# Sliding windows by scatter: identity shuffles in place of VectorE copies, and another buffer for a final tile

## The chip, the cores and the metric

The kernel runs on one core of a Trainium2 chip. The metric is the device time of one execution in microseconds (us), as the median of several runs. Profiles come from one execution each, with all times counted from the start of its span.

## What is computed

The input `x` is 16 x 64 x 64 x 64 float32 (batch, channel, row, column). The output holds, for each of 15 x 15 window positions, the 8 x 8 window of every channel; windows step by 4 rows and columns, so they overlap by half.

```python
n_h = (h - window_size) // stride + 1      # 15
n_w = (w - window_size) // stride + 1      # 15
for i in range(n_h):
    for j in range(n_w):
        result[:, i, j] = x[:, :, 4*i:4*i + 8, 4*j:4*j + 8].copy()
```

Nothing is calculated. The input has 16.8 MB and the output 59.0 MB: 3600 rows (batch, i, j) of 64 x 8 x 8 float32, 16 KB each.

## The kernel before

**Input.** The tile `L` keeps the whole input in the on-chip memory. A partition stands for a half of the channels (`ch`, partitions 0 to 63 or 64 to 127), one of two groups of eight batches (`y`), a batch and a quarter of the image's rows (`q`); it has 32 channels x 16 rows x 64 columns. Sixteen loads of a `(ch, y, q)` each, eight of them split over two queues, are issued by SyncE (SP) and GpSimd (POOL). A window's upper edge lies in one of four slots `s` of a quarter; windows of slots 0 to 2 lie inside the quarter, and those of slot 3 take their lower four rows from the next partition.

**Output tiles.** Four buffers `G0` to `G3` of 128 partitions x 64 x 8 x 8 are used in turn: `tile_()` counts `at` up and gives `G[(at - 1) % 4]`. A tile is filled by copies on ScalarE (`act`) and VectorE (`dve`), each of which takes a strided 8-column piece out of `L`, and is then sent by `scatter` (L123), an indirect DMA on POOL's queue that gives each partition a row of the output by an index tile. Indices beyond the bound mark rows that are left out. A buffer is filled again when its last store has landed, so three tiles can be under way while the fourth is filled.

**The order.** It is written out by hand:

- `part` (L166): six tiles of slots 0 and 1 of two columns of windows, eight copies of 32 partitions each; they need only half of the input (`y`), so that the first three go out while the other half loads.
- `unit(j, 0)`, the plain tile: `fill` makes four copies of 64 partitions x 2048 elements (L143), two on ScalarE and two on VectorE. There are eight, the first three between the later `part` tiles.
- `unit(j, 2)`, the cross tile: one half of the partitions gets slot 2 by two ScalarE copies (L143), the other half gets slot 3 by VectorE: for each channel half a copy of the upper four rows (L145, 64 x 1024) and a `stream_shuffle` of the lower four rows from the next partition (L146, 64 x 1024, mask `nxt`). 16 of its 128 rows are left out. There are 15.
- From the fourth plain tile on three cross tiles and a plain tile alternate, five times.
- At the end the last column's slots 0 and 1 make two tiles of 64 partitions (L212): two copies on ScalarE and two on VectorE fill one, and four plain DMAs of 256 KB (L215) send it. The first tile's four DMAs are on SP's queue, the second's alternate between SP and ScalarE.

Counted from 0, tiles 0 to 8 are the `part` tiles and the first three plain ones, 9 to 28 the five rounds. `at` is 29 then; with the `at += 1` in the final loop, its two tiles get the buffers of tiles 25 and 27 (`G1` and `G3`).

POOL executes its scatters in order, each after the copies that fill its tile. ScalarE and VectorE execute their copies in order and wait, at a tile's first copy, for its buffer's last store. The stores are declared to be independent of each other.

Of the kernel before, what the change touches and what calls it, by code (L numbers as in the profile page):

```python
# [10 lines left out]
def kernel(  # L11
# [7 lines left out]
    nc = tc.nc  # L19
# [11 lines left out]
    CH = 2  # L31
# [6 lines left out]
    HP = P // CH  # L38
# [79 lines left out]
    def free(st):  # L118
        tc.declare_no_dep(st.ins, group="stores", reason="each store writes rows of its own")
        tc.add_to_no_dep_group("stores", st.ins)  # L120

    def scatter(g, ix, j, s):
        st = nc.gpsimd.indirect_dma_start(  # L123
            out=o_v,
            out_offset=bass.IndirectOffsetOnAxis(ap=ix[:, 0:1], axis=0),
            in_=g.rearrange("p c r w -> p (c r w)"),
            in_offset=None,
            element_offset=(s * NW + j) * CFREE,
            bounds_check=B * NWIN - 1,
            oob_is_err=False,  # L130
        )
        free(st)

    def fill(g, half, s, j, lo, n, copies):

        d = slice(half * HP + lo, half * HP + lo + n)
        cols = slice(j * ST, j * ST + WS)
        for ch in (half, 1 - half):
            f = slice(ch * HP + lo, ch * HP + lo + n)
            cs = slice(ch * CL, (ch + 1) * CL)  # L140
            copy = copies[ch != half]
            if s < NSLOT - 1:
                copy(out=g[d, cs, :, :], in_=L[f, :, s * ST : s * ST + WS, cols])  # L143
            else:
                copy(out=g[d, cs, 0:ST, :], in_=L[f, :, s * ST : RB, cols])  # L145
                nc.vector.stream_shuffle(out=g[d, cs, ST:WS, :], in_=L[f, :, 0:ST, cols], mask=nxt)  # L146

    act, dve = nc.scalar.copy, nc.vector.tensor_copy


    EARLY = 3
    at = 0

    def tile_():
        nonlocal at
        at += 1
        return G[(at - 1) % NG]

    def part(y, j):
        g = tile_()  # L160
        for d in range(P // QP):
            s, dj = d // NY, d % NY
            cols = slice((j + dj) * ST, (j + dj) * ST + WS)
            for ch in range(CH):
                f = (ch * NY + y) * QP
                (act if (2 * d + ch) % 3 == 0 else dve)(  # L166
                    out=g[d * QP : (d + 1) * QP, ch * CL : (ch + 1) * CL, :, :],
                    in_=L[f : f + QP, :, s * ST : s * ST + WS, cols],
                )
        scatter(g, (idx_y0, idx_y1)[y], j, 0)  # L170

    crossed = 0

    def unit(j, s):
        nonlocal crossed
        g = tile_()
        if s == 0:
            for half in range(CH):
                fill(g, half, half, j, 0, HP, (act, dve))
            scatter(g, idx, j, s)  # L180
        else:

            turn = crossed % 2
            crossed += 1
            fill(g, turn, s, j, 0, HP, (act, act))
            fill(g, 1 - turn, s + 1, j, 0, HP, (dve, dve))
            scatter(g, (idx_hi, idx_lo)[turn], j, s)

    for n in range(EARLY):
# [1 line left out]
    plain = [(j, 0) for j in range(2 * EARLY, NW - 1)]  # L191
    cross = [(j, 2) for j in range(NW)]
    for n in range(EARLY):
        part(1, 2 * n)
        unit(*plain.pop(0))
    while plain:
        for w in cross[:3]:
            unit(*w)
        cross = cross[3:]
        unit(*plain.pop(0))  # L200


    j = NW - 1
    for s in range(2):
        g = tile_()
        at += 1
        cols = slice(j * ST, j * ST + WS)
        for y in range(NY):
            d = slice(QP + y * QP, QP + (y + 1) * QP)
            for ch, copy in enumerate((act, dve)):  # L210
                f = slice(ch * HP + y * QP, ch * HP + (y + 1) * QP)
                copy(out=g[d, ch * CL : (ch + 1) * CL, :, :], in_=L[f, :, s * ST : s * ST + WS, cols])  # L212
        g_q = g.rearrange("p c r w -> p (c r w)")
        for q in range(HQ):
            free((nc.sync, nc.scalar)[s * q % 2].dma_start(out=o_q[q * NSLOT + s, j], in_=g_q[QP + q : QP + q + (B - 1) * HQ + 1 : HQ]))  # L215
# [35 lines left out]
```

## Time and profile before

| | |
|---|---|
| median of 8 runs | 192.09 us (191.96 to 192.33) |
| the profiled execution | 192.27 us, of which its span is 190.5 |
| scatters (L123) | 29; issue to landing 8.0 to 16.4 us, median 13.7 |
| scatter packets (16 KB) | 3472 |
| ScalarE copy, 2048 elements | 1896 ns |
| VectorE copy of 2048, of 1024 elements | 1225 ns, 688 ns |
| VectorE shuffle of 1024 elements | 1275 ns |
| scatter on POOL | 0.96 to 2.2 us |

A line of the profile's groups names the line of code, the engine, the operation and its output and input with their shapes, then how many there were, their busy time in us and the mean of one in ns, and the idle time of the engine in front of them with what ended most of it. A line of the timeline has the start and the duration in us, the engine, the line and the operation; in brackets the idle time before it and what ended it. "SPq" and "ACTq" are DMA issues on these queues. The DMA row of the page is the mean busy share of 16 DMA engines in 40 equal slices of the span, in tenths, where 9 stands for 90% or more.

### The profile page before, as it was taken

Reading aid. Unit: us, or ns where it says so; the run is one execution under the profiler, and the core shown is the slowest. Engines: PE = TensorE matmul, PEld = TensorE weight load, DVE = VectorE, ACT = ScalarE, POOL = GpSimd, SP = SyncE. Lnnn points to the kernel's source line nnn. Section 1 sums busy time; section 2 is a strip of 40 time slices with the busy share of each in tenths; the row PEclk is TensorE's granted clock in tenths of the full one; section 3 lists DMA queues with packets and bytes.
Section 4 is the critical chain, followed back from the end, with each engine's and each line's share of the span. In section 5 each row is a group of like instructions: output and inputs, shape, how many; then the busy total and the mean of one; then the engine's idle time right before and its main releaser. Section 6 shows DMA issues by size and latency. Waiting matters only on the chain.

```text
span 190.5 us, 481 instructions
## 1 busy us (share of the span) xinstructions
DVE 120.5 (63%) x160; ACT 130.0 (68%) x69; POOL 49.8 (26%) x50
## 2 busy tenths in 40 slices
DVE  4000007999998969877749586795877679455220
ACT  0000007999999979977779589797877979487250
POOL 7402203205635321522322222223122432210000
DMA  2999999999999999999999999999999999999974
GB/s 84 318 405 401 400 399 398 399 400 395 420 437 423 418 420 427 427 403 434 437 403 427 421 421 416 423 430 416 420 423 420 416 427 427 408 423 434 413 337 169
DMA packets 11156, 75.81 MB, mean 398 GB/s; under 512 B 3456, under 2 KB 3456, under 8 KB 7552
## 3 DMA queue, kind: packets, MB, share of 16 engines
q0 software_dynamic: 9040, 66.34, 84.7%
q1 hardware_dynamic: 2048, 8.91, 12.0%
q10 hardware_dynamic: 64, 0.52, 0.7%
q14 instruction: 4, 0.03, 0.0%
HBM read 16.78 MB, written 62.91 MB: 418 GB/s over the span
## 4 chain that ended last, share of the span: by engine, by line
DMA 84%; DVE 6%; ACT 3%; POOL 2%; issue 1%; ACTq 0%; DVEq 0%; PEldq 0%
DMA out_dram<-G,idx_hi 30%; DMA L<-in_x_dram 21%; DMA out_dram<-G,idx 14%; DMA out_dram<-G,idx_y 13%; DMA out_dram<-G,idx_lo 7%; DVE G L166 4%; POOL L L58 2%; ACT G L212 2%; ACT G L143 1%; DVE G L146 1%; DVE G L145 0%; DVE G L143 0%; POOL pi L69 0%; ACTq L143 0%; DVEq L145 0%
## 5 line engine op out<-in xcount | busy, mean ns | idle before, releaser
L143 ACT COPY G<-L 64x2048 f32<-64x2048 f32 x46 | 87.2, 1896 | 16.9 <-DMA out_dram<-G,idx_hi 7.6
L166 DVE COPY G<-L 32x2048 f32<-32x2048 f32 x30 | 36.7, 1222 | 29.3 <-DMA L<-in_x_dram 26.3
L146 DVE STREAM_SHUFFLE G<-L 64x1024 f32<-64x1024 f32 x30 | 38.3, 1275 | 0.0
L166 ACT COPY G<-L 32x2048 f32<-32x2048 f32 x18 | 33.9, 1896 | 1.3 <-DMA out_dram<-G,idx_y 1.0
L145 DVE COPY G<-L 64x1024 f32<-64x1024 f32 x30 | 20.6, 688 | 16.6 <-DMA out_dram<-G,idx_hi 10.4
L143 DVE COPY G<-L 64x2048 f32<-64x2048 f32 x16 | 19.6, 1225 | 6.6 <-DMA out_dram<-G,idx 6.3
L166 ACT ACT_TABLE_LOAD x1 | 1.3, 1283 | 29.8 <-DMA L<-in_x_dram 29.8
L123 POOL DMA_INDIRECT out_dram<-G,idx_y x6 | 10.9, 1810 | 25.1 <-DVE G L166 15.6
L58 POOL DMA_DIRECT2D L<-in_x_dram x16 | 11.0, 696 | 24.4 <-DMA L<-in_x_dram 23.9
L123 POOL DMA_INDIRECT out_dram<-G,idx_hi x8 | 9.6, 1200 | 24.1 <-DVE G L146 15.3
L123 POOL DMA_INDIRECT out_dram<-G,idx_lo x7 | 8.1, 1152 | 29.3 <-DVE G L146 19.6
L123 POOL DMA_INDIRECT out_dram<-G,idx x8 | 10.0, 1254 | 18.3 <-ACT G L143 18.3
L212 ACT COPY G<-L 32x2048 f32<-32x2048 f32 x4 | 7.6, 1896 | 5.5 <-DMA out_dram<-G,idx_hi 5.5
L212 DVE COPY G<-L 32x2048 f32<-32x2048 f32 x4 | 5.1, 1280 | 8.0 <-DMA out_dram<-G,idx_hi 7.9
L72 DVE TENSOR_SCALAR tb<-pi 128x1 int32<-128x1 int32 x1 | 0.2, 153 | 1.0 <-POOL pi L69 1.0
L78 DVE TENSOR_TENSOR th<-tc,tq 128x1 int32<-128x1 int32 x2 | 0.3, 156 | 0.0
L75 DVE TENSOR_SCALAR th<-tc 128x1 int32<-128x1 int32 x2 | 0.3, 154 | 0.0
L69 POOL IOTA pi<- 128x1 int32 x1 | 0.1, 125 | 0.4 <-PEq L246 0.4
L146 DVE LOAD_MASK_SELECT G<-L x30 | 0.2, 7 | 0.0
L78 DVE CUSTOM_DVE_ANT_0 idx_y<-idx_y,idx 128x2 uint16<-128x2 uint16 x1 | 0.2, 159 | 0.0
L78 DVE CUSTOM_DVE_ANT_0 idx_lo<-tb,th 128x2 uint16<-128x2 uint16 x1 | 0.2, 159 | 0.0
L78 DVE CUSTOM_DVE_ANT_0 idx<-tb,th 128x2 uint16<-128x2 uint16 x1 | 0.2, 159 | 0.0
(16 smaller groups left out, 2.2 us busy)
## 6 DMA issues: line engine op xcount, KB each, us to landing
L<-in_x_dram POOLq DMA_DIRECT2D x8, 1024.0 KB, 21.2
L<-in_x_dram SPq DMA_DIRECT2D x8, 896.0 KB
out_dram<-G SPq DMA_DIRECT2D x6, 256.0 KB
L<-in_x_dram POOLq DMA_DIRECT2D x8, 128.0 KB, 21.3
out_dram<-G ACTq DMA_DIRECT2D x2, 256.0 KB
out_dram<-G,idx POOLq DMA_INDIRECT x8, 14.9
out_dram<-G,idx_hi POOLq DMA_INDIRECT x8, 14.6
out_dram<-G,idx_lo POOLq DMA_INDIRECT x7, 12.9
```

The lines of the kernel that those rows point to most:

```text
L58: eng.dma_start(out=L[p0 : p0 + QP - HQ + 1 : HQ, c0:c1, :, :], in_=x_v[ch, y, q, :, c0:c1, :])
L69: nc.gpsimd.iota(pi[:, :], pattern=[[0, 1]], base=0, channel_multiplier=1)
L72: nc.vector.tensor_scalar(out=d[:, :], in0=pi[:, :], scalar1=shift, scalar2=mask, op0=ALU.logical_shift_right, op1=ALU.bitwise_and)
L75: nc.vector.tensor_scalar(out=d[:, :], in0=a[:, :], scalar1=float(m), scalar2=None, op0=ALU.mult)
L78: nc.vector.tensor_tensor(out=d[:, :], in0=a[:, :], in1=b[:, :], op=op)
L123: st = nc.gpsimd.indirect_dma_start(out=o_v, out_offset=bass.IndirectOffsetOnAxis(ap=ix[:, 0:1], axis=0), in_=g.rearrange("p c r w -> p (c ...
L143: copy(out=g[d, cs, :, :], in_=L[f, :, s * ST : s * ST + WS, cols])
L145: copy(out=g[d, cs, 0:ST, :], in_=L[f, :, s * ST : RB, cols])
L146: nc.vector.stream_shuffle(out=g[d, cs, ST:WS, :], in_=L[f, :, 0:ST, cols], mask=nxt)
L166: (act if (2 * d + ch) % 3 == 0 else dve)(out=g[d * QP : (d + 1) * QP, ch * CL : (ch + 1) * CL, :, :], in_=L[f : f + QP, :, s * ST : s * S ...
L212: copy(out=g[d, ch * CL : (ch + 1) * CL, :, :], in_=L[f, :, s * ST : s * ST + WS, cols])
```

## The change

A second VectorE helper moves rows by a shuffle whose mask maps each partition to itself, so that the same data is moved as by a copy. A third, `mix`, gives the first quarter of the channels of a piece to a ScalarE copy and the rest to such a shuffle. In the plain tiles from the fourth on VectorE's two copies of 2048 elements become a shuffle of 2048 and a `mix` (ScalarE 512, VectorE 1536). In the cross tiles VectorE's two copies of 1024 elements become a shuffle of 1024 and a `mix` (ScalarE 256, VectorE 768); the two shuffles with the mask `nxt` stay. The first three plain tiles, the `part` tiles and the final two keep their copies.

The count of buffers at the end changes as well: one buffer is passed over ahead of the final loop and none within it, so that its two tiles get the buffers of tiles 26 and 27 (`G2` and `G3`).

```diff
     act, dve = nc.scalar.copy, nc.vector.tensor_copy
+    same = list(range(32))
+
+
+    def shf(out, in_):
+        nc.vector.stream_shuffle(out=out, in_=in_, mask=same)
+
+    def mix(out, in_):
+        k = out.shape[1] // 4
+        act(out=out[:, 0:k], in_=in_[:, 0:k])
+        shf(out=out[:, k:], in_=in_[:, k:])
...
-    def unit(j, s):
+    def unit(j, s, fast=False):
         nonlocal crossed
         g = tile_()
         if s == 0:
-            for half in range(CH):
-                fill(g, half, half, j, 0, HP, (act, dve))
+            fill(g, 0, 0, j, 0, HP, (act, dve if fast else shf))
+            fill(g, 1, 1, j, 0, HP, (act, dve if fast else mix))
             scatter(g, idx, j, s)
         else:
...
             fill(g, turn, s, j, 0, HP, (act, act))
-            fill(g, 1 - turn, s + 1, j, 0, HP, (dve, dve))
+            fill(g, 1 - turn, s + 1, j, 0, HP, (shf, mix))
             scatter(g, (idx_hi, idx_lo)[turn], j, s)
...
         part(1, 2 * n)
-        unit(*plain.pop(0))
+        unit(*plain.pop(0), fast=True)
...
     j = NW - 1
+    tile_()
     for s in range(2):
         g = tile_()
-        at += 1
         cols = slice(j * ST, j * ST + WS)
```

## The prediction, made before the changed kernel ran

> **What bounds the kernel now.** I read the page's busy line and its 40 slices first, to see which resource is full.
>
> ```profile
> DVE 120.5 (63%) x160; ACT 130.0 (68%) x69; POOL 49.8 (26%) x50
> ...
> DMA  2999999999999999999999999999999999999974
> GB/s 84 318 405 401 400 399 398 399 400 395 420 437 423 418 420 427 427 403 434 437 403 427 421 421 416 423 430 416 420 423 420 416 427 427 408 423 434 413 337 169
> ```
>
> No compute engine is full; the DMA engines are at 9 in every slice between the first and the last two. The windows view of 2 us stretches says whether the dips in GB/s are idle time (columns: length, busy us and count of DVE, ACT and POOL, PEclk, DMA share, GB/s).
>
> ```profile
> 110.00:112.00 2.00, 1.24 (x2) 1.26 (x2) 0.14 (x1) 1.00 1.02 430
> 112.00:114.00 2.00, 1.97 (x2) 1.98 (x2) 1.24 (x1) 1.00 0.99 418
> 114.00:116.00 2.00, 0.57 (x2) 1.88 (x2) 0.07 (x1) 1.00 0.98 401
> 116.00:118.00 2.00, 1.97 (x4) 1.98 (x2) 1.32 (x1) 1.00 1.08 459
> ```
>
> They are not: the share stays within some hundredths of 1.00, and GB/s swings only by which window a 16 KB packet starts in. The trace's DMA records give the 3472 scatter packets 0.611 us at the least and 0.624 on average, with 16 of them in flight on average in every 2 us from 48 to 179 us. The steady part is bound by the transfers. Third, the groups, for the prices:
>
> ```profile
> L146 DVE STREAM_SHUFFLE G<-L 64x1024 f32<-64x1024 f32 x30 | 38.3, 1275 | 0.0
> ...
> L145 DVE COPY G<-L 64x1024 f32<-64x1024 f32 x30 | 20.6, 688 | 16.6 <-DMA out_dram<-G,idx_hi 10.4
> L143 DVE COPY G<-L 64x2048 f32<-64x2048 f32 x16 | 19.6, 1225 | 6.6 <-DMA out_dram<-G,idx 6.3
> ```
>
> VectorE waits for stores to release buffers (10.4 and 6.3 us above), not the stores for VectorE. Last, the timeline, for one plain tile (from 111.84) and for the end (the four large copies of ScalarE at 111.83 are of two tiles).
>
> ```profile
> 111.83 7.76 ACT L143 COPY G<-L 64x2048 f32<-64x2048 f32 x4 [0.74 <-DMA out_dram<-G,idx]
> 111.84 2.52 DVE L143 COPY G<-L 64x2048 f32<-64x2048 f32 x2 [0.76 <-DMA out_dram<-G,idx]
> 111.86 1.39 POOL L123 DMA_INDIRECT out_dram<-G,idx_lo  x1 [4.85 <-ACT G L143]
> ...
> 170.80 0.96 POOL L123 DMA_INDIRECT out_dram<-G,idx  x1 [4.75 <-ACT G L143]
> 171.34 3.82 ACT L212 COPY G<-L 32x2048 f32<-32x2048 f32 x2 [0.81 <-DMA out_dram<-G,idx_hi]
> 171.35 2.71 DVE L212 COPY G<-L 32x2048 f32<-32x2048 f32 x2 [2.15 <-DMA out_dram<-G,idx_hi]
> 175.18 10.28 SPq L215 DMA_DIRECT2D out_dram<-G  x6
> 179.82 3.82 ACT L212 COPY G<-L 32x2048 f32<-32x2048 f32 x2 [4.66 <-DMA out_dram<-G,idx_hi]
> ```
>
> The last scatter (tile 28, counting from 0) is issued at 170.80. The one before it (tile 27, issued 165.09) lands at 179.74, where the final copies begin. Transfers run in order, so tile 28 starts moving at about 179: **8 us of queue** lie between issue and transfer. The trace's landing increments add that eight of a scatter's sixteen come early and eight late (175.6 to 175.9 and 178.8 to 179.7 for tile 27): half the DMA engines lag, and the end is theirs. From 179.3 each of them has 8 + 4 + 4 packets left (tile 28 and the two final tiles), 16 x 0.615 = 9.8 us, which gives 189.1; the last landing is at 189.44.
>
> **Part 1: shuffles for copies.** Of the 23 later tiles the 15 cross tiles and the 5 plain ones outside the first phase change; the first three plain tiles keep their copies. From start to start a 1024-element copy takes 0.62 us and a shuffle 1.29 (the rows at 109.20 and 109.82, and the next start).
> - Cross tile, VectorE before: 2 x (0.62 + 1.29) = 3.82. After: two shuffles of old, 2.58; a new one of 1024, 1.29; a new one of 768 elements. The trace has no 768; the one-element operations take 0.15, so 0.15 + 768/1024 x (1.275 - 0.15) = 0.99, 1.01 with the gap; between 0.96 (in proportion) and 1.29 (no cheaper than 1024). Sum 4.88 (4.83 to 5.16).
> - Plain tile before: 2.47. After: 2048 and 1536 elements, by the same line 2.40 and 1.84, 4.28 with gaps. In proportion to 1024 it would be 4.52, with the 1536 no cheaper than the 2048 5.16; a dearer fixed part pulls it down to 4.2.
> - ScalarE adds a copy of 256 elements in a cross tile, 512 in a plain one. Only 2048 elements are shown, 1896 ns: in proportion 0.24 and 0.47, with VectorE's fixed 0.15 about 0.4 and 0.6, and 1.90 at the very most. Tiles follow every 4.63 us (92.62 to 166.72 for 16), and ScalarE's two large copies use 3.82, so up to some 0.75 us is free. I take 0.4 and 0.6, nearer the proportion, since more elements must cost more.
>
> VectorE then needs 15 x 4.88 + 5 x 4.28 = 94.6 us for twenty tiles, where it needed 15 x 3.82 + 5 x 2.47 = 69.7: **24.9 us more work**. The cover is its own waiting. From its first cross tile at 78.02, with one wait of 0.7 us (tile 13's buffer, free at 97.6), it is through with tile 28 at 78.0 + 94.6 + 0.7 = 173.3; ScalarE was at 170.5. Tile 28's scatter comes at 173.4 in place of 170.8, tile 27's at 169.1 in place of 165.09.
>
> Behind them waits only POOL's queue, and then the transfers. Tile 27 is wanted when tile 26 is done, at 174.1 to 174.9; tile 28 at about 179. The shortest issue to landing of any scatter is 8.0 us, of which some 5.0 are its own eight packets, so issue to first byte is 3.0 at most. The slack left is at least 174.1 - 169.1 - 3.0 = 2 us for tile 27 and 2.6 for tile 28. The queue gets shorter and doesn't run dry: **cost 0**. If that cover goes, each us that tile 28 slips behind 176 (179 less 3.0) is a us of the end.
>
> **Part 2: no large copies beside the descriptor writing.** POOL's scatters take 0.96 us when alone and up to 1.76 beside a VectorE copy (147.44, copy from 147.84); over the steady part the excess above 0.96 is 4.3 us in 12 scatters. By the windows no DMA engine waits for it, so I take 0; the two ends come from the packets. Those wholly under a copy last 0.623 us, wholly under a shuffle 0.626, under neither 0.627: no gain in this row. From both sides, a late DMA engine spends 5.03 us on eight packets in the middle and 5.12 at its worst, a fast one 4.93. Over the some 116 packets that it moves from tile 12 on, that is -1.5 us (4.93) to +1.3 (5.12).
>
> The Trainium skill (SBUF — State Buffer, "SBUF: two separate sides") says that a float32 VectorE copy shuts GpSimd out of a shared port, so that it can't write descriptors and the DMA engines idle; the longer scatters agree, the DMA share of 1.0 doesn't show the idling. By that rule up to those 4.3 us would come back; by the row, none.
>
> **Part 3: the first final tile's buffer.** It moves from the buffer of tile 25 (free at 171.26) to that of tile 26 (174.90). ScalarE's two copies end at 174.95 + 3.82 = 178.8 in place of 175.17, and VectorE's 2.5 fit in. SP's four DMAs take 0.6 + 3 x 1.4 = 4.8 us to issue, so until 183.65 where they ended at 180.0; SP's two of the second tile (ready at 183.65 as before, since tile 27's landing sets it) stand behind them, and the last ends at about 186.4 in place of 185.46. In the trace a store begins to move some 1.0 us after its issue ends: at 187.4. The late engines are busy until 188.5 with the rest, so this costs 0, with 1 us of room. If the room is gone it costs at most the 0.95.
>
> **Part 4: code.** VectorE executes 40 more instructions (mask loads), ScalarE 20 more. The trace has four instruction fetches of 8 KB (62.9, 106.0, 111.8, 165.3), 0.31 us of one DMA engine each; the last leaves one late engine 0.4 us behind its fellows at the end. Moved earlier it gives up to 0.4 back, moved later or joined by another it costs about as much. I take +0.1.
>
> **Sum.** Span 190.5 + 0 + 0 + 0 + 0.1 = 190.6; with the 1.8 that lies outside (192.27 profiled less 190.5) 192.4. The profiled execution is 0.18 above the median of 192.09, so the forecast is **192.2**.
>
> **Rivals.**
> - *VectorE becomes the bound (slower).* For: its busy share rises to about 100% of the steady part, as 3 x 4.88 + 4.28 = 18.9 us stand against 18.5 for four tiles. Against: 2 us or more of queue. By the upper prices (5.16 each) it is through at 78.0 + 20 x 5.16 = 181.2; the late engines get tile 28 at about 183.0 (by 3.0, 184.3), 4 to 5.2 us after they want it: 196 to 197. It decides from tile 28 ready after 176, that is 4.9 us a tile on average where I have 4.77. Its likeliest time is 194, for 5.04 a tile.
> - *Descriptors come sooner and packets shorten (faster).* For: the scatters up to 0.8 longer beside copies. Against: no idle DMA time, no shorter packets outside copies. 192.1 - 1.5 = 190.6.
> - *The end of the two plain tiles slips (slower).* For: SP's queue. Against: the room of 1 us. 192.1 + 0.5, half of 0.95, gives 192.6.
>
> **How the numbers follow.** A difference below 0.2% (0.4 us) can't be told from none here. Forecast, the late DMA engines full throughout: 0.48, of which 0.32 within 0.2%, 0.06 faster and 0.10 slower (part 4, part 2's ends). VectorE bound: 0.16, slower. Shorter packets: 0.20, faster. End slips: 0.16, 0.14 slower and 0.02 same. Together faster 0.26, same 0.34, slower 0.40. The likeliest case alone spans 191.5 to 193.0. For 8 in 10 the range takes in most of the faster rival and VectorE's usual time: 190.8 to 194.2.
>
> **What would show it.** VectorE's new groups at about 1.0, 1.28, 1.84 and 2.40 us; its idle time before them nearly gone; DMA slices still 9; issue to landing of the scatters down from 13 to 15 us to about 10 to 12 near the end; the last scatter at about 173.4; final copies still at about 179.8; scatters all near 0.96. A scatter later than 176, DMA slices under 9, or a second final copy that no longer waits for a landing would make it wrong, and so would packets away from 0.624.

## The result, and the profile after

The changed kernel takes **191.66 us** (median of 12 runs, 191.54 to 192.10) against 192.20 for the kernel before (33 runs, 191.84 to 192.52): ratio 0.9975, 95% interval 0.9967 to 0.9982. It is a quarter of a per cent faster, where no change was forecast. Its profiled execution took 191.60 us, of which 189.8 are its span.

The page of the changed kernel, its busy line and its slices:

```profile
DVE 142.5 (75%) x200; ACT 139.2 (73%) x89; POOL 46.5 (25%) x50
...
DMA  2999999999999999999999999999999999999984
GB/s 84 313 403 402 398 400 397 400 402 401 428 425 432 430 432 421 421 428 418 442 394 433 423 404 439 425 404 425 439 397 432 423 407 425 432 428 404 438 352 176
```

VectorE has 22 us more work (120.5 before), the DMA engines are as full as they were. The windows view of two of the stretches shown before (length, then busy us and count of DVE, ACT and POOL, PEclk, DMA share, GB/s):

```profile
112.00:114.00 2.00, 2.00 (x1) 1.98 (x2) 0.96 (x1) 1.00 1.06 451
114.00:116.00 2.00, 1.96 (x4) 1.98 (x2) 0.00 (x0) 1.00 1.01 418
```

VectorE, which idled for 1.4 of the 2 us from 114 on, is now busy throughout, and the DMA share is about 1.00 as before. The groups, with shapes kept apart:

```profile
L153 DVE STREAM_SHUFFLE G<-L 64x1024 f32<-64x1024 f32 x15 | 19.2, 1282 | 0.5
L153 DVE STREAM_SHUFFLE G<-L 64x768 f32<-64x768 f32 x15 | 15.0, 999 | 0.5
L153 DVE STREAM_SHUFFLE G<-L 64x2048 f32<-64x2048 f32 x5 | 12.1, 2429 | 0.1
...
L153 DVE STREAM_SHUFFLE G<-L 64x1536 f32<-64x1536 f32 x5 | 9.3, 1860 | 0.2
```

The number in front of the last bar of each is the mean in ns: 1282, 999, 2429 and 1860, within 2% of the forecast 1.28, 0.99, 2.40 and 1.84 us. The last number is idle time before them: next to nothing, where the copies of before had 23 us. The timeline at the end:

```profile
168.02 0.96 POOL L123 DMA_INDIRECT out_dram<-G,idx_hi  x1 [3.78 <-ACT G L143]
...
172.36 0.96 POOL L123 DMA_INDIRECT out_dram<-G,idx  x1 [3.38 <-issue]
173.97 3.81 ACT L222 COPY G<-L 32x2048 f32<-32x2048 f32 x2 [3.55 <-DMA out_dram<-G,idx_lo]
...
177.81 7.49 SPq L225 DMA_DIRECT2D out_dram<-G  x6
178.99 3.82 ACT L222 COPY G<-L 32x2048 f32<-32x2048 f32 x2 [1.20 <-DMA out_dram<-G,idx_hi]
```

The last two scatters come 2.9 and 1.6 us later than before (165.09 and 170.80), yet the final copies begin 0.83 us earlier (179.82 before), because tile 27 lands earlier. So the gain is in the transfers, not in what feeds them. The trace's landing increments show where. Each scatter has sixteen, one per DMA engine; the last is one engine's, and I give how far it is behind the fifteenth:

| | tile 19 | tile 20 | tile 23 | tile 24 | tile 27 | final stores |
|---|---|---|---|---|---|---|
| before: fifteenth at | 142.73 | 147.74 | 160.32 | 165.35 | 179.04 | 189.05 |
| before: sixteenth behind it | 0.02 | 0.01 | 0.02 | **1.28** | 0.70 | **0.39** |
| after: fifteenth at | 142.32 | 147.37 | 159.97 | 164.99 | 178.79 | 188.77 |
| after: sixteenth behind it | 0.03 | **1.24** | 0.54 | 0.37 | 0.12 | **0.13** |

One DMA engine falls 1.2 to 1.3 us behind in both, and then makes it good over some six tiles. Before, this happens at tile 24, and there is no time left to make it good; after, at tile 20. The increments do not name their engines; that it is one and the same engine is read from the times. Of the 0.54 us by which the last landing comes earlier (189.44 to 188.90), this engine accounts for 0.26 and the other fifteen for the rest. The window views of the DMA queues show what stands at the places where it falls behind. The kernel before, in the us from 165 to 166:

```profile
q0 software_dynamic: 27, 0.38, 91.2%
q14 instruction: 1, 0.01, 1.9%
```

The changed kernel, in the same us:

```profile
q0 software_dynamic: 29, 0.48, 115.8%
```

and from 147 to 148:

```profile
q0 software_dynamic: 27, 0.39, 100.2%
q14 instruction: 1, 0.01, 1.9%
```

The line `q14 instruction` is one fetch of 8 KB of instructions (its record: 309 ns). Both kernels have four after the start, before at 62.9, 106.0, 111.8 and 165.3 us, after at 62.4, 102.0, 107.1 and 147.2. The last falls at VectorE's 192nd instruction before and its 196th after, counting all that the trace lists for VectorE (205 and 245). The changed kernel's mask loads add two instructions per tile, so VectorE reaches that count four tiles sooner. The Trainium skill (Runtime: NRT & Kernel Launch, "Instruction fetch mechanics") says that the sequencer fetches the next block through a DMA queue of its own while it executes, at a cost that is mostly hidden; the fetches and their queue agree, but what is hidden from VectorE need not be hidden from a store that is queued on the same DMA engine, and an engine is 1.2 to 1.3 us late from there on.

That is an observation in two profiles. The identical opening of the two kernels also differs by 0.3 us (first scatter at 44.81 and 44.47), and that alone is as much as the other fifteen engines gain, so two profiles can't settle what a quarter of a per cent is due to; the timed experiments have to.

### The profile page after: what moved, and what is told of

Read it like the earlier page. It is cut to its first block, busy times and chain, and to the rows that moved or that the text cites. A ratio compares the mean times of both kernels' runs of the same rounds, so it can differ in the third digit from the quotient of the medians.

```text
span 189.8 us, 556 instructions
## 1 busy us (share of the span) xinstructions
DVE 142.5 (75%) x200; ACT 139.2 (73%) x89; POOL 46.5 (25%) x50
## 3 DMA queue, kind: packets, MB, share of 16 engines
q1 hardware_dynamic: 2048, 8.91, 12.1%
## 4 chain that ended last, share of the span: by engine, by line
DMA 55%; DVE 30%; issue 6%; POOL 2%; ACT 2%; DVEq 0%; PEldq 0%; ACTq 0%
DMA L<-in_x_dram 20%; DMA out_dram<-G,idx 15%; DVE G L153 14%; DMA out_dram<-G,idx_hi 13%; DVE G L146 11%; DMA out_dram<-G,idx_y 6%; DVE G L176 5%; POOL L L58 2%; ACT G L222 2%; DVE G L143 0%; DVEq L176 0%; POOL pi L69 0%; DVEq L153 0%; PEldq L256 0%; ACTq L222 0%
## 5 line engine op out<-in xcount | busy, mean ns | idle before, releaser
L153 DVE STREAM_SHUFFLE G<-L 64x1024 f32<-64x1024 f32 (+3 forms) x40 | 55.7, 1392 | 1.3
L123 POOL DMA_INDIRECT out_dram<-G,idx_hi x8 | 7.7, 963 | 30.5 <-DVE G L146 19.2
L123 POOL DMA_INDIRECT out_dram<-G,idx_lo x7 | 6.7, 964 | 27.5 <-DVE G L146 19.0
L157 ACT COPY G<-L 64x256 f32<-64x256 f32 (+1 forms) x20 | 9.1, 456 | 0.5
L143 DVE COPY G<-L 64x2048 f32<-64x2048 f32 x6 | 7.3, 1222 | 0.2
```

The costliest lines, as they stand in the source:

```text
L123: st = nc.gpsimd.indirect_dma_start(out=o_v, out_offset=bass.IndirectOffsetOnAxis(ap=ix[:, 0:1], axis=0), in_=g.rearrange("p c r w -> p (c ...
L153: nc.vector.stream_shuffle(out=out, in_=in_, mask=same)
L157: act(out=out[:, 0:k], in_=in_[:, 0:k])
```

## The experiments

Each was timed in five rounds against the kernel before on the chip that it ran on. The first and the last fetch of each stand in the table behind them.

**e1, the shuffles alone**, with the final buffers of before:

```diff
     j = NW - 1
-    tile_()
     for s in range(2):
         g = tile_()
+        at += 1
```

> The shuffles of the change alone, with the final tiles in the buffers of before (tiles 25 and 27). Code-fetch theory (the last 8 KB fetch moves from 165 to about 147 us, so the one late DMA engine recovers before the end): the whole gain is here, about 0.4 to 0.5 us below before (ratio 0.9975). Descriptor theory (scatters of 0.96 us throughout let the DMA engines do more): the same total, but then the landings of tiles 9 to 24 come at closer spacing than before. Buffer theory (the gain comes from the first plain store starting later): no gain here, ratio 1.000.

Measured: 191.73 us against 192.14, ratio 0.9976 (0.9965 to 0.9987). The whole gain is here. The landings of tiles 9 to 24 take 67.9 us by their fifteenth increments, as in the kernel before and the changed one, so not by a better rate in the middle.

**e2, the buffers alone**, the opposite edit in the kernel before:

> The buffers of the change alone (tiles 26 and 27), with VectorE's copies. Code-fetch and descriptor theories: same as before, ratio 1.000, with the last fetch at about 165 us and the last landing's sixteenth increment some 0.4 us behind the fifteenth. Buffer theory: the whole gain, ratio 0.9975.

Measured: 192.01 us, ratio 0.9995 (0.9985 to 1.0005), last fetch at 165.4 us, the late engine 0.56 us behind at the end. The buffers are worth nothing that can be told from zero.

**e3 and e4, forty and 28 tiny operations during the loads**, in the kernel before and in the changed one:

```diff
+    spare = itile("spare")
+    for n in range(40):
+        mul(spare, pi, 1)
```

> The kernel before, with 40 one-element VectorE operations on a spare tile while the input loads (VectorE idles there from 3.6 to 29.9 us), so that VectorE's count of instructions is that of the changed kernel and its code fetches come earlier; copies, buffers and order as before. Code-fetch theory: the last fetch leaves 165 us (to about 130), the late engine recovers, 0.3 to 0.5 us faster, ratio about 0.998. Descriptor and buffer theories: ratio 1.000, since neither copies nor buffers change.

> The changed kernel with 28 such operations during the loads, so that VectorE's 256th instruction, and with it one more code fetch, comes at about 165 us. Code-fetch theory: the late engine is 0.9 to 1.3 us behind at tile 24 or 25 again and the gain is lost, ratio to before about 1.000. Descriptor and buffer theories: the gain stays, ratio 0.9975.

Measured: e3 191.98 us, ratio 0.9991 (0.9983 to 1.0000), and e4 191.50 us, ratio 0.9966 (0.9955 to 0.9977). e3 gained less than I expected although its last fetch went to 139.4 us and its late engine was 0.06 us behind at the end. Its first fetch had gone to 13.5 us, into the loads; whether that is why is taken up with e9. e4 missed its aim: no fetch came at the 256th of its 273 listed instructions; the last came at the 192nd, at 128.3 us. It is one more case of an early last fetch.

**e5, the changed kernel with a late fetch**, by 28 such operations and 64 more:

```diff
+    for n in range(64):
+        mul(spare, pi, 1)
```

> The changed kernel with 28 one-element VectorE operations during the loads and 64 more behind its last copy, in VectorE's idle time, so that there is code left to fetch when VectorE comes to its 256th instruction, at about 165 us. Code-fetch theory: a fetch at 165 us, a late engine 0.9 to 1.3 us behind at tile 24 and some 0.4 us at the end, ratio to before 0.999 to 1.000. Shuffle theory (the shuffles bring the gain in another way): ratio 0.997 to 0.998 whatever the fetch.

Measured: 192.39 us against 192.33, ratio 1.0002 (0.9993 to 1.0012). The gain is gone, with every shuffle in place. The fetch came at 165.9 us and the late engine was 1.1 us behind at tile 25 and 0.66 at the end. However, the 64 operations, which depend on nothing, were placed at the front of VectorE's queue: all 92 ran between 1.3 and 18.6 us, and another fetch fell at 10.2 us.

**e6, copies kept, more VectorE work and more instructions:**

```diff
-                nc.vector.stream_shuffle(out=g[d, cs, ST:WS, :], in_=L[f, :, 0:ST, cols], mask=nxt)
+                for _ in range(1 + (ch == half)):
+                    nc.vector.stream_shuffle(out=g[d, cs, ST:WS, :], in_=L[f, :, 0:ST, cols], mask=nxt)
```

> The kernel before, with one of the two nxt shuffles of each cross tile issued twice: VectorE's copies stay, but it has 1.29 us more work in a cross tile (3.82 to 5.11), so its scatters are late about as in the changed kernel, and 30 more instructions, so its last code fetch comes before 165 us. Code-fetch theory: 0.1 to 0.4 us faster. Descriptor theory (it is the copies beside the scatters): ratio 1.000. Late-scatter theory (a shorter queue of descriptors is what helps): ratio 0.998.

Measured: 191.62 us against 192.33, ratio 0.9963 (0.9950 to 0.9975). Its groups:

```profile
L147 DVE STREAM_SHUFFLE G<-L 64x1024 f32<-64x1024 f32 x45 | 57.7, 1281 | 1.1
...
L145 DVE COPY G<-L 64x1024 f32<-64x1024 f32 x30 | 20.6, 688 | 3.2 <-DMA out_dram<-G,idx_hi 1.4 <-DMA out_dram<-G,idx_y 1.0
```

All thirty copies are there, and the scatters are as long beside them as before: 5.8 us in excess of 0.96 each over the last 21 scatters, against 4.4 before and 0.06 after. The whole gain comes without one identity shuffle. That speaks against the descriptor theory as the cause. What it shares with the changed kernel is later scatters and an earlier last fetch (156.0 us, first fetch unmoved at 62.6). But it is no clean case of the code-fetch theory: its 0.7 us are more than the 0.1 to 0.4 expected, and its late engine is still 0.64 us behind at tile 27 and 0.52 at the end, more than in the kernel before. Its other fifteen engines are early: tiles 9 to 24 take 67.5 us by their fifteenth increments, where the kernel before, the changed one and e1 take 67.9. Where that comes from is not shown.

**e9, copies and earlier fetches**, by 36 of the small operations:

> The kernel before, with 12 one-element VectorE operations behind each of the first three plain tiles (55 to 78 us, so after the loads), none during the loads; copies, buffers and order stay. VectorE comes to its 192nd instruction about 27 us sooner, at about 138 us. Code-fetch theory: no fetch at 165 us, the late engine level with its fellows at the end, 0.3 to 0.6 us faster, ratio 0.997 to 0.9985, as with shuffles. Rival (e3 showed nearly all that a fetch is worth, the rest is the later scatters'): ratio 0.999 to 1.000.

Measured: 191.66 us against 192.20, ratio 0.9970 (0.9961 to 0.9980). The operations ran from 1.3 to 8.1 us, not where the expectation has them; the first fetch came at 33.6 us, the last at 142.3, and the late engine ended 0.01 us behind. Copies and buffers are those of before, the scatters are as long (4.3 us in excess of 0.96 each over the last 21; the last at 169.5 us, 170.8 before), and **the time is the changed kernel's**. The operations move both of VectorE's fetches, the first and the last. The window of the last, from 142 to 143 us:

```profile
q0 software_dynamic: 31, 0.38, 91.4%
q14 instruction: 1, 0.01, 1.9%
```

e9 differs from e3 by four operations out of forty. The four put the first fetch of e3 to 13.5 us:

```profile
q1 hardware_dynamic: 37, 0.12, 30.2%
q14 instruction: 1, 0.01, 1.9%
...
L<-in_x_dram SPq DMA_DIRECT2D x1, 896.0 KB
```

That is e3's window from 13 to 14 us: the fetch stands beside the queue of the input loads (q1), and the last line is a load issued in it. e9's window from 33 to 34 us, with its own first fetch:

```profile
q1 hardware_dynamic: 42, 0.17, 45.9%
q14 instruction: 1, 0.01, 2.1%
```

The intervals of e3 and e9 don't overlap, so e3 lacks some 0.2%. That the fetch at 13.5 us is the reason is not shown: e9's stands beside the loads too, and e5, which has a fetch at 10.2 us besides one at 165.9, is no slower than the kernel before, which has the late one alone (1.0012 at most).

**e10, shuffles and late fetch:** the changed kernel with 94 of the operations.

> The changed kernel, with 10 such operations behind each of the first three plain tiles and 64 behind VectorE's last copy, so that a code fetch falls at about 164 us, and none more during the loads. Code-fetch theory: the gain is gone or nearly gone, ratio 0.999 to 1.000, without the extra fetch during the loads that e5 had. Rival (e5 lost its gain to the fetch during the loads): ratio 0.9975.

Measured: 192.38 us against 192.20, ratio 1.0011 (1.0001 to 1.0021), fetches at 10.5 and 166.0 among others. All 94 ran between 1.3 and 19.0 us, so this repeats e5 rather than parting its two fetches, and "none more during the loads" did not come true. The loss against the changed kernel, 0.36%, is the two fetches together; the profiles part them, in the table below.

**e12, most copies gone, the fetches unmoved:**

```diff
-            fill(g, 1 - turn, s + 1, j, 0, HP, (dve, dve))
+            fill(g, 1 - turn, s + 1, j, 0, HP, (shf, act))
```

> The kernel before, with the two copies of each cross tile replaced by a shuffle of 1024 elements on VectorE and a copy of 1024 on ScalarE: thirty of the forty copies beside the scatters are gone, VectorE has as many instructions as before (a mask load and a shuffle for two copies), and no operation is added, so the code fetches keep their places (one at about 165 us, none between 5 and 60). Buffers of before, plain tiles with copies. Code-fetch theory: ratio 0.999 to 1.001, the late engine again some 0.4 us behind at the end. Descriptor theory: most of the gain, ratio 0.9975 to 0.9985.

Measured: 191.89 us against 192.07, ratio 0.9991 (0.9981 to 1.0001). Its groups and, below, its DMA queues from 164 to 166 us:

```profile
L153 DVE STREAM_SHUFFLE G<-L 64x1024 f32<-64x1024 f32 x15 | 19.3, 1285 | 0.3
L145 ACT COPY G<-L 64x1024 f32<-64x1024 f32 x15 | 15.6, 1043 | 0.3
```

```profile
q0 software_dynamic: 64, 0.79, 96.7%
q14 instruction: 1, 0.01, 1.0%
```

The cross tiles have no VectorE copy left (ScalarE took fifteen, shuffles the other fifteen), the last fetch is at 164.7 us, and the gain is not there; at most 0.2% by the interval. The late engine was 1.07 us behind at tile 28 and 0.63 at the end, more than the expected 0.4. With e9 this makes a cross: copies with an early fetch gain, shuffles with a late one don't. It does not test the descriptor theory, though, because its scatters are no shorter:

```profile
L123 POOL DMA_INDIRECT out_dram<-G,idx_hi x8 | 10.1, 1264 | 31.7 <-ACT G L145 27.7 <-DVE G L143 3.9
L123 POOL DMA_INDIRECT out_dram<-G,idx x8 | 10.0, 1256 | 12.9 <-ACT G L143 12.9
```

The means were 1200 and 1254 ns before; beside the copies of the plain and final tiles six of the last 21 scatters have 5.0 us of excess, against 4.4 before. Against that theory stand e9 and e6, which have the long scatters and the gain.

**e7, e8 and e11, which half of the DMA engines is the late one.** The flip spares the lower partitions in eight cross tiles and the upper in seven:

```diff
-            turn = crossed % 2
+            turn = (crossed + 1) % 2
```

> The kernel before, with the first cross tile leaving out rows of the lower half, so that eight of the fifteen cross tiles spare the lower partitions and seven the upper. Theory that the late half of the DMA engines alone sets the end: this half has two packets of 0.62 us less on each engine, the other two more; 0.6 to 1.2 us faster, ratio 0.994 to 0.997, and the two halves land the last store within 0.5 us of each other. Rival (the end is set by the last copies and the issue of the plain stores): ratio 1.000.

> The changed kernel with the same flip. If the end is the late half's, the flip gives what it gives to the kernel before, so 190.5 to 191.0 us, ratio 0.991 to 0.995 to before. If VectorE's later scatters begin to starve the half that is now served first, the gain is smaller than in e7.

> Copies as before, the flip of e7 and the operations of e9 together. Code-fetch theory: copies with the fetch moved are worth as much as the shuffles, so this is at the 190.2 us of e8, ratio 0.989 to 0.991. Rival (the shuffles themselves help): it stays near e7's 191.0, ratio 0.992 to 0.994.

Measured: e7 (before) 190.96 us, ratio 0.9930 (0.9917 to 0.9942); e8 (after) **190.16 us, ratio 0.9895** (0.9880 to 0.9911); e11 (before, with e9's operations) 190.31 us, ratio 0.9898 (0.9883 to 0.9914). The flip gives 1.4 us, a little more than two packets of 0.62 us. In the profiles the early half lands its last final store at 187.87 and the late one at 189.44 in the kernel before, at 187.16 and 188.17 in e7, at 186.74 and 187.40 in e8: still not level, but closer; in e7 they are 1.0 us apart where 0.5 was expected, 0.45 of it by the one late engine. e8 beats both kernels. e11 is within 0.0003 of it with VectorE's copies, so again copies with earlier fetches do as well as the shuffles, within intervals of 0.003.

| run | VectorE's cross-tile copies | first, last fetch (us) | late engine behind at the end (us) | first scatter to last landing (us) | ratio (95%) |
|---|---|---|---|---|---|
| before | yes | 62.9, 165.3 | 0.39 | 144.63 | 1 |
| e2 | yes | 63.0, 165.4 | 0.56 | 144.71 | 0.9995 (0.9985 to 1.0005) |
| e12 | no | 62.3, 164.7 | 0.63 | 144.75 | 0.9991 (0.9981 to 1.0001) |
| e10 | no | 10.5, 166.0 | 0.64 | 144.67 | 1.0011 (1.0001 to 1.0021) |
| e5 | no | 10.2, 165.9 | 0.66 | 144.64 | 1.0002 (0.9993 to 1.0012) |
| e3 | yes | 13.5, 139.4 | 0.06 | 144.19 | 0.9991 (0.9983 to 1.0000) |
| e6 | yes | 62.6, 156.0 | 0.52 | 144.31 | 0.9963 (0.9950 to 0.9975) |
| after | no | 62.4, 147.2 | 0.13 | 144.43 | 0.9975 (0.9967 to 0.9982) |
| e1 | no | 62.8, 147.6 | 0.06 | 144.29 | 0.9976 (0.9965 to 0.9987) |
| e9 | yes | 33.6, 142.3 | 0.01 | 144.21 | 0.9970 (0.9961 to 0.9980) |
| e4 | no | 38.6, 128.3 | 0.12 | 144.29 | 0.9966 (0.9955 to 0.9977) |

The late engine is again the sixteenth increment behind the fifteenth, of the store that lands last. The next column runs from the issue of the first scatter to the last landing, in one profile of each run; it leaves out the opening, by which profiles differ (first scatter at 44.3 to 44.9 us). By it the runs part without exception, with copies and without in both groups: a last fetch near 165 us gives 144.63 to 144.75 us, one at 156 us or sooner 144.19 to 144.43. e5 and e10 are in the first group, so their late fetch costs 0.2 to 0.4 us here against the changed kernel, e1 and e4, without the one among the loads. e3 is in the second, as short as e9; what it lacks in the timed runs is not found behind its first scatter, in the one execution that was profiled (191.78 us, its fastest). Only e6 is short with its engine still late.

The ratios part the runs in the same way but for e3: 0.996 to 0.998 with an early last fetch, 0.999 to 1.001 for all others. A fetch during the first 20 us sets e3 apart from the rest of its group, but this bound was drawn after the results were seen.

## Why the prediction was wrong

**What bounds the kernel: right.** The transfers do, and the late half of the engines sets the end; the flip, which moves nothing but packets between the halves, shows it by 1.4 us.

**Part 1, cost 0: right.** VectorE's new pieces were priced within 2%, ScalarE's at 403 and 617 ns for the 0.4 and 0.6 taken. A cross tile takes VectorE 4.75 us (120.64 to 125.39) for the 4.88 forecast, so the last scatter is at 172.36, not 173.4. The queue held. The page's chain of waits of the changed kernel runs through VectorE for 30% of the span (6% before), which looks like the rival's bound. It follows a landing back to its scatter's issue and from there to VectorE, past the time in which the scatter only queues; e9, with VectorE idle as before, is not faster than the changed kernel.

**Part 2, cost 0: right,** and the row decided rightly against the rule. The scatters did become 0.96 us each, which took away the 4.3 us of excess, and no gain of their own shows: e9 has the gain with the excess still there, and e5 and e10 have no excess and no gain. The 16 KB packets that start between 100 and 180 us last 0.624 us on average in both kernels (the least of all is 0.608 before, not 0.611; nothing rests on it). The rival that had the right sign, shorter packets, had this mechanism, and it fell with e6 and e9. Whether shuffles add up to 0.1 or 0.2% of their own is open, since e12's interval leaves room for it.

**Part 3, cost 0: right** within e2's interval; in the changed kernel SP's last issue ended at 185.30 us, not at the 186.4 forecast.

**Part 4, "I take +0.1": the term that failed.** The fetch at 165.3 us and the engine that it left 0.4 us behind were in the text, and so was "moved earlier it gives up to 0.4 back". I treated its new place as unknown, although it could be counted: VectorE's last fetch falls at its 192nd listed instruction in the kernel before, and the edit adds two instructions to each of the tiles in front of it, so it moves by some four tiles to about 147 us, not to a later time. With -0.4 for +0.1 the sum is 191.7, and 191.66 was measured. That it fits so closely is partly luck: the interval of the ratio is 0.35 to 0.63 us, and the late engine accounts for 0.26 us in the two profiles. The edit that moves the fetches and keeps the copies (e9) measured -0.54 us, 192.20 to 191.66. The range began at 190.8 and held the time; what failed is the direction, by the sign of one small term in a sum of zeros.

What is not settled: why a fetch whose record lasts 0.31 us puts its engine 0.8 to 1.5 us back, why e3 gained less than e9, and why e6 gained as much with its engine still late; its later scatters are one candidate, though in the changed kernel and e1 later scatters leave tiles 9 to 24 at 67.9 us.

## What to carry to other kernels

When the transfers are full to the last microsecond, everything else that uses a DMA engine counts, and here the instruction stream did: count the instructions up to each fetch and see whether one falls in the last tiles, before a small gain is put down to the work that was edited. A variant that adds instructions should be compared with one that adds the same number of idle ones. And look at the sixteen landings of a store, not at the last: where halves of them drift apart, moving rows from one half to the other can be worth more than the whole change (here 0.7% against 0.25%).

## What had not been expected of the hardware

A code fetch of 8 KB fell at VectorE's 192nd to 199th listed instruction in every run, and in e5 and e10 (there at 92 us) one more at the 319th or 321st of 337 and 339. The first after the start falls at its 62nd to 70th, so VectorE's fetches lie 125 to 136 instructions apart, and e4's 256th was the wrong place to expect one. The two fetches between 101 and 113 us keep their time whatever VectorE's count is (its 111th to 221st), so they are probably other engines'. The fetch at the 192nd to 199th set one DMA engine back by 0.8 to 1.5 us at the next landings, and this engine then caught up at some 0.1 to 0.4 us a tile. And tiny operations with no dependence ran at the front of VectorE's queue, between 1.3 and 19.0 us in every run that has them: a test that wants them at a certain time has to tie them to something that happens then.
